# A two-layer decoder trunk on one core: gates read by ScalarE, eleven projections per layer summed in one PSUM bank

## The chip, the cores and the metric

The kernel runs on one core of a Trainium2 chip. TensorE (PE in the profile) multiplies, VectorE (DVE) and ScalarE (ACT) do the elementwise work, GpSimd (POOL) does a little of it, and SyncE (SP) issues most of the transfers. The metric is device time in microseconds (us) of one execution, as the median of several runs. Before the change it is 1203.29 us, the median of 3 runs that lie between 1203.06 and 1203.56.

## The reference

A batch of one sequence of 256 tokens with 1024 channels goes through two layers, in fp32. What matters here:

```python
for l in range(2):
    h = h + 0.5 * swiglu(rms_norm(h, ffn1_norm[l]), ...)          # 1024 -> 2816 -> 1024
    h = h + mixer(rms_norm(h, mix_norm[l]), ...)                   # four head groups, below
    h = h + cross_attention(rms_norm(h, ...), rms_norm(mem, ...))  # 4 heads of 256
    h = h + 0.5 * swiglu(rms_norm(h, ffn2_norm[l]), ...)
return rms_norm(h, final_norm)

def mixer(u):
    z = u @ w_in
    qa, ka, va, oa, ia, fa, pb, qc, kc, vc, qd, kd, vd = split(z)  # 256 wide, ia and fa 4 wide
    # mLSTM: q, k = silu(causal_conv4([qa | ka]));  i = ia + b;  f = log_sigmoid(fa + b);
    #        chunked recurrence over q, k, va, normalised, times sigmoid(oa)
    # pool:  trailing-window means of pb, minus pb, a 64x64 map per group
    # dilated attention on qc, kc, vc;  differential attention on qd, kd, vd
    return concat([ya, yb, yc, yd]) @ w_out
```

Cross attention needs `K` and `V` from `mem`; the kernel computes these inside the mixer's stretch.

## The kernel before, in words

**Weights.** All weights lie in one array, in the order in which they are used, cut into slabs of 128 x 1024 numbers (1040 where four gate columns are added). SP loads a slab into a `raw` tile. ScalarE copies it, rounded, into the high half of a `whl` tile (the cast, L221), and VectorE puts the remainder into the low half (L222). There are five `whl` buffers, so the cast of a slab needs the buffer of the slab five places earlier, and waits until TensorE has made the last product with that. Five slabs are held ahead of or under TensorE, and casts and remainders come in slab order.

**Products.** Activations are kept as a high and a low part too, and a product is high x high + high x low + low x high. `mm2` does it with two matmuls: one 512 columns wide (L366, the weight's high part against both parts of the activation, which fills two halves of a PSUM bank) and one 256 wide (L367). `mm3` does it with three matmuls 256 wide (L360 to L362), all added up in the same 256 columns. The columns streamed are the same, 768.

**Projections.** `proj_T` (L402) computes one unit of 256 output channels or several together: two slabs each, 16 `mm2` each, into a PSUM tile `pj` of two banks. The pool of `pj` tiles has two buffers. After a unit's second slab, `join` adds the two halves: ScalarE copies one half out (L374, tile `jn`), VectorE adds the other (L375), and with that the PSUM tile is free. `proj_M` (L416) does the same with tokens on the partitions; the units `va+ia` and `oa+fa` are 260 columns wide there (L429) and have their last four columns for the gates. Small products go into `pq` tiles, of which there are four.

**The norm.** Rows of a norm are scaled late: `rstd` (L322 ff.) adds up squares (L329), sums them over partitions by matmul (L335), scales on VectorE (`ms`, L339) and takes the power on GpSimd (`r_tok`, L340). `row_bcast` spreads the result over the partitions by two matmuls (L347), and ScalarE copies them out as `rb` (L352). These steps hang in a list, `later`, of which `proj_T` and `proj_M` run one entry after each slab (`flush`). In an FFN's first group the list holds two empty entries, then `rstd`; in the mixer, two empty ones and `rstd`, then, behind the units `qa` and `ka`, the function `go`, which calls `row_bcast` and multiplies `qa` and `ka` by `rb` (L749).

**The mixer's order.** `MIX_ORDER` (L38) is a list of unit and step names in which the program is written: `qa` and `ka` are computed together, then `va+ia`, `oa+fa`, `qd`, `kd`, `vd` and so on; `conv` is the causal convolution of `qa` and `ka` (L829, L832, then Silu on ScalarE, L835), `gates` the log-sigmoid (L844 to L851, with a table load on ScalarE, L845), `rows` the prefix sums by matmul (L858 to L861), `ds`, `df`, `dp` and `cs`, `cf`, `cp` scores, transposes ("flips") and products of the two attentions. A scheduler of the framework then places the instructions of each engine, so an engine's order differs from the written one in places. Within an engine the order is fixed before the run.

**The start.** The channel table `ch` and the four pieces of `x` (tile `h`) come by two DMA queues, and ScalarE loads its first function table (L282). Fourteen matmuls on zeros (L449) precede the first real one.

Of the kernel before, what the change touches and what calls it, by code (L numbers as in the profile page):

```python
# [14 lines left out]
ALU = mybir.AluOpType  # L15
# [21 lines left out]

MIX_ORDER = """qa  ka  va+ia conv  oa+fa gates  qd  kd rows  vd cols  qc mem ms0 ms1 ds0  kc mp0 ms2 ds1 df0  # L38
    vc mp1 ms3 dp0  pb df1 mp2 mp3 mout ds2  K0 pool ds3 dp1 mgain  K1 df2 cs0  K2 mback dp2 df3 cs1 cf0
    K3 dp3 dout cs2 cf1 cp0 pout  V0 dgain cs3 cf2 cp1  V1 dback cf3 cp2  V2 cp3 cout""".split()  # L40

# [202 lines left out]
def trunk(ctx: ExitStack, tc: tile.TileContext, xT, memT, wall, chan, gateb, dlam, t5, poolw, c128, small, out):  # L244
# [156 lines left out]

    def proj_T(units, l, x, evac):  # L402

        ps_ = [pproj() for _ in units]
        for i in range(2):
            for u, p in zip(units, ps_):
                w = W.get(u, l, i, 256)
                for kk in range(4):
                    k = 4 * i + kk
                    for n in range(2):  # L410
                        mm2(p[:, n * 512:n * 512 + 512], parts(w, kk, slice(n * 128, n * 128 + 128)), x(k), k == 0, k == KD - 1)
                flush()
                if i == 1:
                    evac(u, join(p))

# [55 lines left out]
    def ffn(l, name, norm, c_next, extra=()):  # L471
# [218 lines left out]
    def mixer(l, norm, c_next):  # L690
# [43 lines left out]
        def emit(u):  # L734
# [3 lines left out]
            if u in ("qa", "pb"):  # L738
# [20 lines left out]
            elif u in ("qd", "kd", "qc", "kc"):  # L759
# [3 lines left out]
                def ev(_, p):  # L763
# [4 lines left out]
                    else:  # L768
                        V.tensor_tensor(out=pair(t[:, 0:512]), in0=pair(p[:, 0:512]), in1=twice(rb), op=ALU.mult)
                proj_T(["z:" + u], l, xk, ev)  # L770
                z[u] = t
# [10 lines left out]
            elif u == "va+ia":  # L782
# [5 lines left out]
                for b in range(2):  # L788
                    S.activation(out=va[:, b, :, 0:64], in_=o[b][:, 0:256].rearrange("p (a b) -> p a b", a=4), func=AF.Copy,
                                 scale=r[:, b:b + 1])  # L790
                    V.scalar_tensor_tensor(out=ig[:, b, :], in0=o[b][:, 256:260], scalar=r[:, b:b + 1], in1=gb[:, l, 0:4],
                                           op0=ALU.mult, op1=ALU.add)
                z["va"], z["ig"] = va, ig
            else:
# [6 lines left out]
                with tc.high_priority():  # L801
                    for b in range(2):

                        S.activation(out=sg[:, b * 256:b * 256 + 256], in_=o[b][:, 0:256], func=AF.Tanh, scale=rh[:, b:b + 1])
                        V.scalar_tensor_tensor(out=fg[:, b, :], in0=o[b][:, 256:260], scalar=r[:, b:b + 1], in1=gb[:, l, 4:8],  # L805
                                               op0=ALU.mult, op1=ALU.add)
                z["sg"], z["fg"] = sg, fg
# [13 lines left out]

        def mlstm_conv():
            cv = []
            for u, j2 in (("qa", 0), ("ka", 1)):
                c = ztile("cv")
                for a in range(2):
                    j = 2 * j2 + a
                    dst = c[:, a * 256:a * 256 + 256]
                    V.tensor_scalar(out=dst, in0=z[u][:, a, 0:256], scalar1=gcol(cb + C_CONVW, j), scalar2=gcol(cb + C_CONVB, j),  # L829
                                    op0=ALU.mult, op1=ALU.add)  # L830
                    for i in range(1, 4):
                        V.scalar_tensor_tensor(out=dst, in0=z[u][:, a, i:i + 256], scalar=gcol(cb + C_CONVW + 4 * i, j),  # L832
                                               in1=dst, op0=ALU.mult, op1=ALU.add)
                s = ztile("cs")
                S.activation(out=s[:, 0:512], in_=c[:, 0:512], func=AF.Silu)  # L835
                cv.append(s)
            z["qs"], z["ks"] = cv

# [254 lines left out]
        def kv_unit(u):  # L1093
# [5 lines left out]
            if u[0] == "K":  # L1099
                proj_T(["kv:" + u], l, mk, ev)  # L1100
            else:
                ev(u, proj_M("kv:" + u, l, mk, 256))

        steps = {"conv": mlstm_conv, "gates": mlstm_gates, "rows": mlstm_rows, "cols": mlstm_cols, "mout": mlstm_out, "mgain": mlstm_gain, "dgain": diff_gain,
                 "mback": mlstm_back, "dout": diff_out, "dback": diff_back, "cout": dil_out, "pool": pool, "pout": pool_out,
# [127 lines left out]
```

## Time and profile before

| | |
|---|---|
| median of the runs (lowest to highest) | 1203.29 us (1203.06 to 1203.56) |
| the profiled execution, its own time | 1203.03 us |
| its span, first to last instruction | 1201.2 us |
| mean granted TensorE clock, as a share of full speed | 0.998 |
| PE busy | 1185.6 us, 99% |
| DVE busy | 860.1 us, 72% |
| ACT busy | 690.3 us, 57% |
| POOL busy | 55.4 us, 5% |

All times below are microseconds from the start of the span. A line of the timeline gives an instruction's start, its duration, its engine, its line in the kernel, its operation, the tiles it writes and reads, and in brackets how long the engine was idle before it and what ended that. Matmuls overlap: the distance from one start to the next is what a matmul costs, and the duration shown is longer.

### The profile page before, as it was taken

The page shows a single profiled execution, that of the slowest core. Times are in us where ns is not written, and L with a number is a line of the kernel's source. Part 1 is how long each engine was busy: PE and PEld are TensorE (multiplying, and loading weights), DVE is VectorE, ACT ScalarE, POOL GpSimd, SP SyncE. Part 2 cuts the span into 40 slices and gives each one's busy share as a digit, 9 for nine tenths or more (in the row PEclk, how much of TensorE's full clock was granted, in tenths as well). Part 3 has the DMA queues.
Part 4 walks back from the last instruction along what each step waited for, and adds up shares of the span by engine and source line. Part 5 has one row for each costly group of instructions (what it writes and reads, how often), then busy time and mean ns, then how long its engine had stood idle before and what let it go on. Part 6 is the DMA issues. An engine that isn't in the chain of part 4 may idle for free.

```text
span 1201.2 us, 18655 instructions
## 1 busy us (share of the span) xinstructions
PE 1185.6 (99%) x7248; PEld 1048.3 (87%) x7248; DVE 860.1 (72%) x1250; ACT 690.3 (57%) x1035; POOL 55.4 (5%) x69
## 2 busy tenths in 40 slices
PE   8999999999999999999999999999999999999997
PEld 6888888888898988888888888897888999888886
DVE  7787667869667577775677776686785767777653
ACT  7666556556555565554555555555665655655542
POOL 2100000104000000000000000001120000000000
PEclk9999999999999999999999999999999999999999
DMA  8766765554445356666656566655544534555651
GB/s 294 274 212 187 228 189 184 159 175 154 137 152 174 121 193 194 191 183 198 188 181 194 183 194 226 191 177 145 187 142 151 182 124 157 184 195 183 194 191 37
DMA packets 63033, 216.50 MB, mean 180 GB/s; under 512 B 7712, under 2 KB 8112, under 8 KB 62944
## 3 DMA queue, kind: packets, MB, share of 16 engines
q1 hardware_dynamic: 61056, 211.25, 55.3%
q0 software_dynamic: 1024, 2.80, 0.7%
q8 instruction: 57, 0.93, 0.3%
q10 hardware_dynamic: 864, 1.25, 0.3%
q14 instruction: 32, 0.26, 0.1%
HBM read 210.01 MB, written 2.11 MB: 177 GB/s over the span
## 4 chain that ended last, share of the span: by engine, by line
PE 90%; DVE 7%; issue 1%; ACT 1%; DMA 1%; SPq 0%; POOLq 0%; DVEq 0%
PE pj L366 50%; PE pj L367 26%; PE pj L360 3%; PE pj L361 3%; PE pj L362 3%; DVE whl L222 2%; DVE cv L832 1%; ACT whl L221 1%; DMA raw<-in_wall_dram 1%; DVE att L956 1%; PE pq L362 0%; PE pq L360 0%; PE pq L361 0%; PE pq L895 0%; PE pq L966 0%
## 5 line engine op out<-in xcount | busy, mean ns | idle before, releaser
L366 PE MATMUL pj<-xs,whl 128*128 128x512 f32 x1760 | 615.2, 393 | 2.9 <-DVE fg L805 1.7
L222 DVE TENSOR_TENSOR whl<-raw,whl 128x1024 fp32r<-128x1024 f32 (+1 forms) x391 | 473.8, 1215 | 170.4 <-ACT whl L221 165.2
L221 ACT CAST whl<-raw 128x1024 fp32r<-128x1024 f32 (+1 forms) x391 | 406.8, 1042 | 192.5 <-PE pj L367 110.6
L367 PE MATMUL pj<-xs,whl 128*128 128x256 f32 x1760 | 492.6, 280 | 0.2 <-DVE whl L222 0.2
L366 PEld LDWEIGHTS pj<-xs,whl 128*128 128x128 f32 x1760 | 330.3, 188 | 75.3 <-PE pj L367 2.3
L367 PEld LDWEIGHTS pj<-xs,whl 128*128 128x128 f32 x1760 | 332.5, 189 | 1.6 <-issue 0.9
L366 PE MATMUL pj<-fs,whl 128*128 128x512 f32 x660 | 229.2, 392 | 0.0
L374 ACT COPY jn<-pj 128x512 f32<-128x512 f32 x145 | 85.0, 586 | 194.2 <-PE pj L367 194.2
L367 PE MATMUL pj<-fs,whl 128*128 128x256 f32 x660 | 184.7, 280 | 0.0
L375 DVE TENSOR_TENSOR jn<-pj,jn 128x512 f32<-128x512 f32 x145 | 99.9, 689 | 110.1 <-ACT jn L374 109.7
L366 PEld LDWEIGHTS pj<-fs,whl 128*128 128x128 f32 x660 | 123.9, 188 | 27.2
L367 PEld LDWEIGHTS pj<-fs,whl 128*128 128x128 f32 x660 | 124.7, 189 | 0.0
L366 PE MATMUL pj<-whl,ms 128*128 128x512 f32 x128 | 45.9, 400 | 0.0
L366 PE MATMUL pj<-ms,whl 128*128 128x512 f32 x128 | 45.8, 399 | 0.0
L340 POOL TENSOR_TENSOR r_tok<-ms,nhalf 128x2 f32<-128x2 f32 x10 | 7.9, 788 | 800.3 <-DVE ms L339 800.3
L478 ACT ACTIVATE jn<-jn 128x512 f32<-128x512 f32 x44 | 27.8, 633 | 20.0 <-DVE jn L477 19.8
L486 ACT CAST fs<-jn 128x512 fp32r<-128x512 f32 x44 | 27.4, 622 | 19.5 <-DVE jn L483 19.5
L300 ACT ACTIVATE xs<-h,ch 128x256 fp32r<-128x256 f32 x64 | 29.4, 502 | 13.3 <-DVE h L571 8.5
L360 PE MATMUL pj<-ys,whl 128*128 128x256 f32 x128 | 36.1, 282 | 0.3 <-DVE h L571 0.2
L360 PE MATMUL pj<-os,whl 128*128 128x256 f32 x128 | 35.8, 283 | 0.4 <-DVE h L571 0.4
L361 PE MATMUL pj<-os,whl 128*128 128x256 f32 x128 | 35.9, 281 | 0.2
L367 PE MATMUL pj<-whl,ms 128*128 128x256 f32 x128 | 35.9, 280 | 0.0
(269 smaller groups left out, 1361.6 us busy)
## 6 DMA issues: line engine op xcount, KB each, us to landing
raw<-in_wall_dram SPq DMA_DIRECT2D x377, 512.0 KB, 4.0
raw<-in_wall_dram SPq DMA_DIRECT2D x8, 520.0 KB, 3.9
mem<-memd SPq DMA_DIRECT2D x8, 256.0 KB, 4.8
raw<-in_wall_dram SPq DMA_DIRECT2D x6, 256.0 KB, 4.9
mem<-in_memT_dram SPq DMA_DIRECT2D x4, 256.0 KB, 6.9
br<-drow POOLq DMA_DIRECT2D x4, 256.0 KB, 7.3
memd<-mem POOLq DMA_DIRECT2D x4, 256.0 KB, 4.5
qds<-qdh SPq DMA_DIRECT2D x16, 64.0 KB, 2.0
```

Source lines behind the costliest of these rows:

```text
L221: self.nc.scalar.copy(out=hi[:, a:a + m], in_=r[:, a:a + m])
L222: self.last = self.nc.vector.tensor_tensor(out=lo[:, a:a + m], in0=r[:, a:a + m], in1=hi[:, a:a + m].bitcast(F32), op=ALU.subtract)
L300: S.activation(out=hi, in_=src, func=AF.Copy, scale=gcol(c, k))
L360: PE.matmul(o, w(0), x[:, 0, :], start=first, stop=False, skip_group_check=True)
L361: PE.matmul(o, w(0), x[:, 1, :], start=False, stop=False, skip_group_check=True)
L362: PE.matmul(o, w(1), x[:, 0, :], start=False, stop=last, skip_group_check=True)
L366: PE.matmul(o.rearrange("p (s t) -> p s t", s=2), w(0), x, start=first, stop=False, skip_group_check=True)
L367: PE.matmul(o[:, 0:256], w(1), x[:, 0, :], start=False, stop=last, skip_group_check=True)
L374: S.copy(out=tv, in_=v[:, :, 1, :])
L375: V.tensor_tensor(out=tv, in0=v[:, :, 0, :], in1=tv, op=ALU.add)
L478: S.activation(out=gate[:, 0:512], in_=gate[:, 0:512], func=AF.Silu)
L486: S.copy(out=part(f, 0), in_=pair(up[:, 0:512]))
```

## The change

The change has five parts.

1. **Gates.** The four gate columns of `va+ia` and `oa+fa` are read from PSUM by ScalarE (a copy with a scale, two for each unit), and VectorE adds the bias for both token blocks in one instruction from SBUF. Before, two VectorE instructions for each unit read PSUM (L791, L805).
2. **Order of the mixer.** `conv` becomes `cq` (behind `oa+fa`) and `ck` (behind `qd`), with `gates` behind it; `mem` moves behind `kc`; `pool` moves from behind `K0` to behind `K3`, and `pout` behind `V0`.
3. **One bank.** `proj_T` gets `whole=True` for `qa`, `ka`, `pb`, `qd`, `kd`, `qc`, `kc`, `K0` to `K3`, that is for 11 units in each layer: `mm3` instead of `mm2`, both halves of the unit in one bank, and no `join`. What follows reads PSUM: the multiplications by `rb` (L749, L766, L769) and the splits of `K` (L392, L393).
4. **Start.** The table load and the three pieces of `x` on ScalarE's queue keep their written order, `ch`, table, pieces.
5. **FFN.** In the first group of every FFN, `rstd` comes one slab later (three empty entries instead of two).

```diff
-MIX_ORDER = """qa  ka  va+ia conv  oa+fa gates  qd  kd rows  vd cols  qc mem ms0 ms1 ds0  kc mp0 ms2 ds1 df0
+MIX_ORDER = """qa  ka  va+ia  oa+fa cq  qd ck gates  kd rows  vd cols  qc ms0 ms1 ds0  kc mem mp0 ms2 ds1 df0
...
             nc.scalar.dma_start(out=ch[:], in_=chan)
-        q.dma_start(out=h[:, 2 * j:2 * j + 2, :], in_=xT[:, 512 * j:512 * j + 512].rearrange("p (a b) -> p a b", a=2))
+            tc.keep_in_program_order(S.preload_act_table_set("silu_and_others"))
+        tc.keep_in_program_order(q.dma_start(out=h[:, 2 * j:2 * j + 2, :],
+                                             in_=xT[:, 512 * j:512 * j + 512].rearrange("p (a b) -> p a b", a=2)))
         W.load()
-    tc.keep_in_program_order(S.preload_act_table_set("silu_and_others"))
...
-    def proj_T(units, l, x, evac):
+    def proj_T(units, l, x, evac, whole=False):
...
-                        mm2(p[:, n * 512:n * 512 + 512], parts(w, kk, slice(n * 128, n * 128 + 128)), x(k), k == 0, k == KD - 1)
+                        ws = parts(w, kk, slice(n * 128, n * 128 + 128))
+                        if whole:
+                            mm3(p[:, n * 256:n * 256 + 256], ws, x(k), k == 0 and n == 0, k == KD - 1 and n == 1)
+                        else:
+                            mm2(p[:, n * 512:n * 512 + 512], ws, x(k), k == 0, k == KD - 1)
                 flush()
                 if i == 1:
-                    evac(u, join(p))
+                    evac(u, p if whole else join(p))
...
-                later.extend([lambda: None] * 2)
+                later.extend([lambda: None] * 3)
                 later.append(lambda: rbs.append(norm.rstd()))
...
-                proj_T(list(tvs), l, xk, got.__setitem__)
+                proj_T(list(tvs), l, xk, got.__setitem__, whole=True)
...
-                        V.scalar_tensor_tensor(out=fg[:, b, :], in0=o[b][:, 256:260], scalar=r[:, b:b + 1], in1=gb[:, l, 4:8],
-                                               op0=ALU.mult, op1=ALU.add)
+                        S.activation(out=fg[:, b, :], in_=o[b][:, 256:260], func=AF.Copy, scale=r[:, b:b + 1])
+                V.tensor_tensor(out=fg[:], in0=fg[:], in1=gb[:, l:l + 1, 4:8].to_broadcast([128, 2, 4]), op=ALU.add)
...
-        def mlstm_conv():
+        def mlstm_conv(u, j2, name):
```

The new lines shift the numbering: L347 of before is L348 after, L352 is L353, L360 to L362 are L361 to L363, L429 is L435, L749 is L755.

The first place is the passage from `qa` and `ka` to `va+ia` in layer 0. On TensorE before, behind the last product of `ka` (L366, L367), the first 24 matmuls of `va+ia` stand ahead of the two that spread the norm:

```order
L366 MATMUL pj<-xs,whl 128x512
L367 MATMUL pj<-xs,whl 128x256
L366 MATMUL pj<-xs,whl 128x512
L367 MATMUL pj<-xs,whl 128x256
L429 MATMUL pj<-whl,xs 128x260 x24
L347 MATMUL pq<-cc,r_tok 128x128 x2
L429 MATMUL pj<-whl,xs 128x260 x72
```

and now:

```order
L361 MATMUL pj<-xs,whl 128x256
L362 MATMUL pj<-xs,whl 128x256
L363 MATMUL pj<-xs,whl 128x256
L348 MATMUL pq<-cc,r_tok 128x128 x2
L435 MATMUL pj<-whl,xs 128x260 x96
```

The two spreading matmuls (L347, now L348) have moved ahead of all matmuls of `va+ia` and `oa+fa` (96 for both).

On ScalarE at the same place before, with the casts of weights for `oa+fa` (1040 wide) and `qd` (the first 1024 wide one behind them), the joins of `qa` and `ka`, and `rb`:

```order
L221 CAST whl<-raw 128x1040 x2
L300 ACTIVATE xs<-h,ch 128x256 x2
L323 ACTIVATE sq<-h 128x512
L221 CAST whl<-raw 128x1040
L374 COPY jn<-pj 128x512
L221 CAST whl<-raw 128x1040
L374 COPY jn<-pj 128x512
L221 CAST whl<-raw 128x1024 x2
L352 COPY rb<-pq 128x256
```

and now:

```order
L221 CAST whl<-raw 128x1040 x2
L301 ACTIVATE xs<-h,ch 128x256 x2
L324 ACTIVATE sq<-h 128x512
L221 CAST whl<-raw 128x1040 x2
L221 CAST whl<-raw 128x1024
L353 COPY rb<-pq 128x256
L221 CAST whl<-raw 128x1024
```

The joins are gone, and one cast for `qd` still stands ahead of `rb`.

On VectorE at the same place before, from the norm's `ms` to the convolution:

```order
L339 TENSOR_SCALAR ms<-pq 128x2
L800 TENSOR_SCALAR rh<-r_tok 128x2
L375 TENSOR_TENSOR jn<-pj,jn 128x512
L222 TENSOR_TENSOR whl<-raw,whl 128x1040
L375 TENSOR_TENSOR jn<-pj,jn 128x512
L222 TENSOR_TENSOR whl<-raw,whl 128x1024 x2
L749 TENSOR_TENSOR qa<-jn,rb 128x2x256
L749 TENSOR_TENSOR ka<-jn,rb 128x2x256
```

and now:

```order
L340 TENSOR_SCALAR ms<-pq 128x2
L806 TENSOR_SCALAR rh<-r_tok 128x2
L222 TENSOR_TENSOR whl<-raw,whl 128x1040
L222 TENSOR_TENSOR whl<-raw,whl 128x1024
L755 TENSOR_TENSOR qa<-pj,rb 128x2x256
L755 TENSOR_TENSOR ka<-pj,rb 128x2x256
L222 TENSOR_TENSOR whl<-raw,whl 128x1024
```

The multiplications that take `qa` and `ka` out of PSUM now stand behind one remainder for `qd` instead of two, and the joins ahead of them are gone.

The second place is VectorE in the first group of the first FFN, where `jn` is first the gate unit, then the up unit. Before:

```order
L222 TENSOR_TENSOR whl<-raw,whl 128x1024 x2
L329 TENSOR_TENSOR acc<-acc 128x256
L375 TENSOR_TENSOR jn<-pj,jn 128x512
L339 TENSOR_SCALAR ms<-pq 128x2
L222 TENSOR_TENSOR whl<-raw,whl 128x1024
L375 TENSOR_TENSOR jn<-pj,jn 128x512
L222 TENSOR_TENSOR whl<-raw,whl 128x1024 x2
L477 TENSOR_TENSOR jn<-jn,rb 128x512
```

and now:

```order
L222 TENSOR_TENSOR whl<-raw,whl 128x1024 x2
L376 TENSOR_TENSOR jn<-pj,jn 128x512
L222 TENSOR_TENSOR whl<-raw,whl 128x1024
L330 TENSOR_TENSOR acc<-acc 128x256
L376 TENSOR_TENSOR jn<-pj,jn 128x512
L340 TENSOR_SCALAR ms<-pq 128x2
L222 TENSOR_TENSOR whl<-raw,whl 128x1024 x2
L483 TENSOR_TENSOR jn<-jn,rb 128x512
```

The sum of squares (`acc`) and `ms` have moved behind one more remainder and behind the joins.

## Rows read from the trace of the kernel before

**Rows 1.** The page, part 1: busy us (share of the span) and instructions

```profile
PE 1185.6 (99%) x7248; PEld 1048.3 (87%) x7248; DVE 860.1 (72%) x1250; ACT 690.3 (57%) x1035; POOL 55.4 (5%) x69
```

**Rows 2.** Waits of PE: us in total, times, longest

```profile
PE pj L366 <- DVE fg L805: 1.7, 2, 0.8
PE pq L966 <- DVE nm L956: 1.3, 2, 0.7
```

**Rows 3.** Timeline of PE, last slab of ka (mm2): start, duration, operation

```profile
206.62 0.40 PE L366 MATMUL pj<-xs,whl 128*128 128x512 f32 x1
...
208.71 0.39 PE L366 MATMUL pj<-xs,whl 128*128 128x512 f32 x1
...
209.05 3.04 PE L429 MATMUL pj<-whl,xs 128*128 128x260 f32 x24
211.93 0.61 PE L347 MATMUL pq<-cc,r_tok 128*128 128x128 f32 x4
212.29 1.93 PE L429 MATMUL pj<-whl,xs 128*128 128x260 f32 x14
```

**Rows 4.** Timeline of PE, output projection (mm3)

```profile
332.44 0.28 PE L362 MATMUL pj<-ys,whl 128*128 128x256 f32 x1
...
335.57 0.28 PE L362 MATMUL pj<-ys,whl 128*128 128x256 f32 x1
...
337.70 0.28 PE L362 MATMUL pj<-ys,whl 128*128 128x256 f32 x1
```

**Rows 5.** Timeline of ACT behind ka

```profile
209.25 0.59 ACT L374 COPY jn<-pj 128x512 f32<-128x512 f32 x1 [1.68 <-PE pj L367]
...
212.17 1.05 ACT L221 CAST whl<-raw 128x1024 fp32r<-128x1024 f32 x1 [1.38 <-issue]
213.13 0.36 ACT L352 COPY rb<-pq 128x256 f32<-128x256 f32 x1
```

**Rows 6.** Timeline of DVE behind ka

```profile
213.25 1.22 DVE L222 TENSOR_TENSOR whl<-raw,whl 128x1024 fp32r<-128x1024 f32 x1 [1.20 <-ACT whl L221]
214.40 0.69 DVE L749 TENSOR_TENSOR qa<-jn,rb 128x512 f32<-128x512 f32 x1
```

**Rows 7.** Timeline of PE, from qd to kd in layer 0

```profile
226.44 0.28 PE L367 MATMUL pj<-xs,whl 128*128 128x256 f32 x1
227.57 0.47 PE L366 MATMUL pj<-xs,whl 128*128 128x512 f32 x1 [0.85 <-DVE fg L805]
```

**Rows 8.** Timeline of PE, at a flip of layer 0

```profile
297.90 0.28 PE L367 MATMUL pj<-ms,whl 128*128 128x256 f32 x1
298.85 0.55 PE L966 MATMUL pq<-cc,e 128*128 128x128 f32 x3 [0.67 <-DVE nm L956]
```

**Rows 9.** Timeline of ACT, the gates' table load in layer 0

```profile
227.19 1.28 ACT L845 ACT_TABLE_LOAD   x1
```

**Rows 10.** Timeline of PE, first group of the first FFN

```profile
19.30 0.28 PE L367 MATMUL pj<-xs,whl 128*128 128x256 f32 x1
20.22 0.58 PE L335 MATMUL pq<-ones,acc 128*128 128x1 f32 x4 [0.65 <-ACT jn L374]
...
23.62 0.60 PE L347 MATMUL pq<-cc,r_tok 128*128 128x128 f32 x4
```

**Rows 11.** Timeline of DVE in the same stretch

```profile
17.39 2.35 DVE L222 TENSOR_TENSOR whl<-raw,whl 128x1024 fp32r<-128x1024 f32 x2
```

**Rows 12.** Timeline of POOL in the same stretch

```profile
21.15 1.56 POOL L340 TENSOR_TENSOR r_tok<-ms,nhalf 128x2 f32<-128x2 f32 x1 [19.41 <-DVE ms L339]
```

**Rows 13.** Timeline of ACT at the start

```profile
5.22 0.51 ACT L300 ACTIVATE xs<-h,ch 128x256 fp32r<-128x256 f32 x1 [1.31 <-DMA ch<-in_chan_dram]
6.23 0.62 ACT L221 CAST whl<-raw 128x512 fp32r<-128x512 f32 x1 [0.50 <-DMA raw<-in_wall_dram]
```

**Rows 14.** Timeline of PE at the start, matmuls on zeros

```profile
1.32 2.31 PE L449 MATMUL pj<-warm 128*128 128x512 bf16 x5 [1.32 <-POOL nhalf L291]
...
4.95 1.24 PE L449 MATMUL pj<-warm 128*128 128x512 bf16 x5
```

More of the change, by code (lines that the diff above doesn't have):

```diff
@@ L36 @@
 OUT_ORDER = [0, 1, 2, 3, 6, 7, 4, 5]
-MIX_ORDER = """qa  ka  va+ia conv  oa+fa gates  qd  kd rows  vd cols  qc mem ms0 ms1 ds0  kc mp0 ms2 ds1 df0
-    vc mp1 ms3 dp0  pb df1 mp2 mp3 mout ds2  K0 pool ds3 dp1 mgain  K1 df2 cs0  K2 mback dp2 df3 cs1 cf0
-    K3 dp3 dout cs2 cf1 cp0 pout  V0 dgain cs3 cf2 cp1  V1 dback cf3 cp2  V2 cp3 cout""".split()
+MIX_ORDER = """qa  ka  va+ia  oa+fa cq  qd ck gates  kd rows  vd cols  qc ms0 ms1 ds0  kc mem mp0 ms2 ds1 df0
+    vc mp1 ms3 dp0  pb df1 mp2 mp3 mout ds2  K0 ds3 dp1 mgain  K1 df2 cs0  K2 mback dp2 df3 cs1 cf0
+    K3 pool dp3 dout cs2 cf1 cp0  V0 dgain cs3 cf2 cp1 pout  V1 dback cf3 cp2  V2 cp3 cout""".split()
 C_PER_LAYER = 66
@@ L769, in ev @@
                         V.tensor_tensor(out=pair(t[:, 0:512]), in0=pair(p[:, 0:512]), in1=twice(rb), op=ALU.mult)
-                proj_T(["z:" + u], l, xk, ev)
+                proj_T(["z:" + u], l, xk, ev, whole=True)
                 z[u] = t
@@ L790, in emit @@
                                  scale=r[:, b:b + 1])
-                    V.scalar_tensor_tensor(out=ig[:, b, :], in0=o[b][:, 256:260], scalar=r[:, b:b + 1], in1=gb[:, l, 0:4],
-                                           op0=ALU.mult, op1=ALU.add)
+                    S.activation(out=ig[:, b, :], in_=o[b][:, 256:260], func=AF.Copy, scale=r[:, b:b + 1])
+                V.tensor_tensor(out=ig[:], in0=ig[:], in1=gb[:, l:l + 1, 0:4].to_broadcast([128, 2, 4]), op=ALU.add)
                 z["va"], z["ig"] = va, ig
@@ L820, in group_rms @@
             return rs
-        def mlstm_conv():
[L823 to L837, printed above, removed]
+        def mlstm_conv(u, j2, name):
+            c = ztile("cv")
+            for a in range(2):
+                j = 2 * j2 + a
+                dst = c[:, a * 256:a * 256 + 256]
+                V.tensor_scalar(out=dst, in0=z[u][:, a, 0:256], scalar1=gcol(cb + C_CONVW, j), scalar2=gcol(cb + C_CONVB, j),
+                                op0=ALU.mult, op1=ALU.add)
+                for i in range(1, 4):
+                    V.scalar_tensor_tensor(out=dst, in0=z[u][:, a, i:i + 256], scalar=gcol(cb + C_CONVW + 4 * i, j),
+                                           in1=dst, op0=ALU.mult, op1=ALU.add)
+            s = ztile("cs")
+            S.activation(out=s[:, 0:512], in_=c[:, 0:512], func=AF.Silu)
+            z[name] = s
         def mlstm_gates():
@@ L1099, in kv_unit @@
             if u[0] == "K":
-                proj_T(["kv:" + u], l, mk, ev)
+                proj_T(["kv:" + u], l, mk, ev, whole=True)
             else:
                 ev(u, proj_M("kv:" + u, l, mk, 256))
-        steps = {"conv": mlstm_conv, "gates": mlstm_gates, "rows": mlstm_rows, "cols": mlstm_cols, "mout": mlstm_out, "mgain": mlstm_gain, "dgain": diff_gain,
+        steps = {"cq": lambda: mlstm_conv("qa", 0, "qs"), "ck": lambda: mlstm_conv("ka", 1, "ks"), "gates": mlstm_gates, "rows": mlstm_rows, "cols": mlstm_cols, "mout": mlstm_out, "mgain": mlstm_gain, "dgain": diff_gain,
                  "mback": mlstm_back, "dout": diff_out, "dback": diff_back, "cout": dil_out, "pool": pool, "pout": pool_out,
```

1 line of the change is left out of this document (removed).

## Prediction

> **What bounds the kernel now.** I read the page's first part first: TensorE is busy 99% of the span, VectorE 72%, ScalarE 57% [rows 1]. So a microsecond is gained or lost only where TensorE waits, or where it issues more. Next the list of what TensorE waits for: the two entries that the change can touch come twice each, once for each layer: a matmul of a projection behind the forget gate `fg`, and a flip behind the row maxima `nm` of the differential scores [rows 2]. Last the timelines around those places and around the places where the order of instructions has changed. TensorE's own rate is read as distances between starts: six `mm2` of `ka`'s last slab run from 206.62 to 208.71, 0.348 us each [rows 3]; fifteen `mm3` of the output projection from 332.44 to 337.70, 0.351 each, the last six of them, from 335.57, 0.355 each [rows 4].
>
> The sum is made for the profiled execution, 1203.03 us (span 1201.2 and 1.8 around it). The median shown, 1203.29, lies 0.26 above it, and that is added at the end. A difference under 0.2%, 2.4 us, I count as no change.
>
> **Part by part, in the order of their weight.**
>
> *One bank, and what it holds up.* The joins go: 11 copies and 11 additions per layer on ScalarE and VectorE. That is work beside TensorE, and worth nothing unless one of them was late. But a join also freed a `pj` tile early. For ten of the eleven units what follows is an instruction that is ready to read PSUM at once, and only one unit at a time holds a buffer. `qa` and `ka` differ: they are computed together, hold both buffers of the pool, and their reader, L749, needs `rb`, the spread norm. In the kernel before, `join` has released `ka` by the addition that follows the copy at 209.25 [rows 5], `va+ia` starts without a gap at 209.05 in the buffer of `qa`, the spreading matmuls run inside it at 211.93 [rows 3], and `qa` is only multiplied at 214.40 [rows 6], out of `jn`, where nothing is held up. In the changed kernel `va+ia` needs the buffer of `qa`, so all its matmuls wait for that multiplication. The order agrees: the two spreading matmuls now stand ahead of the first of them.
>
> How long that takes: ScalarE learns of the end of `ka` at 209.25, when its copy starts [rows 5]. That copy is gone, and what starts at that moment is the cast of the first slab of `qd`: the five `whl` buffers make it wait for just this slab of `ka`. It stands ahead of `rb`, and VectorE's remainder for it stands ahead of the multiplication.
> - cast, 1.05 [rows 5]: to 210.30
> - remainder, which starts 0.03 behind a cast's end (212.17 and 1.05 against 213.25) and lasts 1.22 [rows 5, 6]: to 211.55
> - multiplication of `qa`, which starts 0.07 before the end of the remainder ahead of it, and lasts 0.69 [rows 6]: 211.48 to 212.17; `rb` (0.36, behind the cast) is ready by then
> - the first matmul of `va+ia`: some 0.04 later, 212.21, where it was 209.05.
>
> Of these 3.16 us the two spreading matmuls take 0.36, from 211.93 to 212.29, which they took before too, inside `va+ia` [rows 3]. So TensorE stands still for 2.8 us longer than before. This hits each layer once: **+5.5 us** with 2.75 each. Bounds: if `rb` were served first, it would still need the way from the spreading matmuls to its copy, 211.93 to 213.13 [rows 3, 5], 0.36 for the copy and 0.69 for `qa`: from 209.2 to about 211.5, a stall of some 2.0 less the matmuls, 1.9 a layer. From above, another remainder ahead of it would make it 2.8 + 1.2 = 4.0. So 3.8 to 8.0 for both, and I take 5.5, which the order as it stands gives.
>
> *Three matmuls for two.* Each unit has 16 products, so 11 units have 176 in a layer and 352 in all. By the 15 products of [rows 4] one costs 0.003 us more, by the last six 0.007: +1.0 to +2.5 us. I take **+1.3**, near the longer count. The weight loads of the third matmul lie under the one before, as in [rows 4], where three loads run with three matmuls.
>
> *Gates.* A gap in [rows 7]: 226.44 to 227.57 is 1.13 where 0.12 is normal, 1.01 lost, in both layers [rows 2]. `kd` waits there for the buffer of `oa+fa`, which VectorE frees late: its reads of the gates stand behind the convolution and two remainders, and hold up ScalarE's second half of `oa` as well. Now ScalarE alone frees it, while `qd` (5.6 us of products) runs. **−2.0 us**; nothing of it stays, since 5.6 us are a lot against two short reads and a cast of 1.05. The price of the same edit is that the log-sigmoid comes later: `gates` now stands behind `ck`, whose Silu must come before the table load of 1.28 [rows 9]. By my count of VectorE's and ScalarE's orders behind that, `lf` is ready about 25.6 us after `va+ia` starts, and the matmul that reads it, in the midst of `vd`, is reached after 25.4. This is an estimate from durations like those of [rows 5, 6]; I put +0.25 a layer, **+0.5** (0 to 1.2).
>
> *The flip.* From 297.90 to 298.85 TensorE loses 0.83 [rows 8], in both layers [rows 2], because VectorE does a remainder (as long as in [rows 6], 1.22) and a join before the row maxima that free a `pq` tile. The join of `K` is gone, an addition as long as the multiplication of [rows 6], 0.69, and the pool's multiplications come later. What is late next are the row sums and copies for the same flip, ready about when TensorE wants them. **−1.5** for both (0 to −1.7).
>
> *The FFN's norm one slab later.* In the first FFN, TensorE waited at 19.30 for the sum of squares: 20.22 less 19.30 and less the normal 0.12 is 0.80. With the sum later, it goes on to the next slab, but that starts the second half of the gate unit's buffer turn: it waits for the gate unit's join, now behind two remainders that end at 19.74 [rows 11]. TensorE goes on at about 20.4, and after nine more matmuls (1.57) stands at the column sums at 21.95. From there to the end of the power on GpSimd took 20.22 to 22.71 before, 2.49 us [rows 10, 12], the power alone 1.56. So `r_tok` is there at 24.44, and the spreading matmuls, which now follow only seven matmuls later, start at 24.48 instead of 23.62 [rows 10]: **+0.86**. In the other three FFNs GpSimd's power is short (the waits list has no entry for it), and the wait is hidden by seven or eight products: 0, up to +1.2 in each if VectorE takes one remainder first. I keep 0 as the value and 1.2 for the range.
>
> *Order of the start.* ScalarE waits for `ch` until 5.22 in any case, and then for a weight piece 0.50 [rows 13]. The table load fits before that; the pieces of `x` are issued 1.28 later (a table load's duration, [rows 9]) and have slack by my reading of their arrivals. 0, between −0.5 (the weights' first pieces come sooner) and +1.28.
>
> *Pool and `mem`.* They move work of VectorE, GpSimd and the transfer queue across a stretch where no wait of TensorE is listed other than the flip. 0.
>
> **Sum:** 5.5 + 1.3 − 2.0 + 0.5 − 1.5 + 0.9 = +4.7. 1203.03 + 4.7 = 1207.7; against the median 1203.29, 1208.0. Its own range goes from the stall's lower bound, 1.7 less, and `lf` in time, 0.5 less (1205.8), to a second remainder and dearer products, 2.5 + 1.2 more, cut to 1211 since both at once are unlikely.
>
> **The rivals.**
> - *The new stall isn't there, and the waits are gone.* If `va+ia` starts on time, 1203.29 + 4.7 − 5.5 = 1202.5, no change; if `mm3` costs no more than `mm2` too and the first FFN loses nothing, 1200.3, faster by 0.25%. For it: the waits of [rows 2] do end with what the change takes away. Against it: two tiles in a pool of two, both read only after `rb`. It decides by whether the first matmul of `va+ia` runs before L755 has read `qa`. Chance 0.05 for faster.
> - *A short stall.* ScalarE and VectorE get to `rb` and `qa` sooner than the order suggests, by the lower bound of 1.9 a layer, and `lf` comes in time: 1208.0 − 1.7 − 0.5 = 1205.8, and with the flip fully hidden 1205.6, about the edge of no change. Chance 0.13.
> - *The clock falls in the new gap.* [...] Against it: the longest gaps inside the work before, 1.0 us [rows 7], cost nothing beyond themselves, and the mean clock of the run is 0.998; but no gap of 2.8 us is there to read. [...] Chance 0.10.
>
> **Chances.** The forecast with its range 0.72, a short stall 0.13, the clock 0.10, faster 0.05. The short stall's time is at the edge of no change, and I leave most of it there. So slower by over 0.2%: 0.82; within 0.2%: 0.13; faster: 0.05. The range goes from 1205.2, which leaves out the first rival and part of the second, to 1211.6, which takes in the clock.
>
> **What would show it.** In the timeline of the changed kernel the first L435 behind the last slab of `ka` has an idle time of 2.5 to 3 us in both layers, ended by VectorE's L755; the starts of `mm3` products of `qa` lie 0.351 to 0.355 apart; no wait behind `fg` ahead of `kd`; at the flips no wait, or one of a tenth; the first L348 starts near 24.5. If the gap behind `ka` is missing or under 1.5 us, or TensorE's matmuls behind it are twice as far apart as elsewhere, the forecast is wrong. If the time comes out below 1205 with the gap there, then a gain that I put at 0 was not nothing, most likely among the casts and remainders that the joins delayed.

## The result: 1215.04 us, slower by 1%

| | before | changed |
|---|---|---|
| median (lowest to highest) | 1203.17 us (1203.02 to 1203.56, 4 runs) | 1215.04 us (1214.72 to 1216.25, 4 runs) |
| profiled execution, its span | 1203.03 us, 1201.2 | 1215.22 us, 1213.4 |
| mean granted TensorE clock | 0.998 | 0.995 |

The ratio is 1.0099 (95% interval 1.0086 to 1.0111). The direction was forecast, the size was not: +11.9 us against +4.7, outside the range.

The page's first part for the changed kernel, which answers to [rows 1]:

```profile
PE 1190.4 (98%) x7600; PEld 1067.9 (88%) x7600; DVE 850.1 (70%) x1224; ACT 678.5 (56%) x1021; POOL 53.9 (4%) x69
```

VectorE and ScalarE have 10 and 12 us less to do, and TensorE 352 instructions more, the third matmul of each product. TensorE is busy for 4.8 us more, and its idle time (span less busy time) grew from 15.6 to 23.0. The list of its waits, in place of [rows 2]:

```profile
PE pj L435 <- DVE qa L755: 5.4, 2, 2.7
PE pq L861 <- DVE lf L854: 4.5, 2, 2.3
PE pq L348 <- POOL r_tok L341: 1.8, 2, 1.1
PE pj L367 <- DVE jn L376: 1.5, 1, 1.5
```

The two old entries, `fg` and the row maxima, are gone. In their place stand the wait for `qa` that the prediction named, a wait for `lf` of nearly the same size that it put at a quarter of a microsecond a layer, and two waits of the first FFN. (Of the 1.8 for `r_tok`, 1.1 is the final norm's and stood there before as well.)

**The gap behind `ka`.** TensorE's timeline in layer 0, at the place of [rows 3]:

```profile
210.43 0.28 PE L363 MATMUL pj<-xs,whl 128*128 128x256 f32 x1
210.55 0.61 PE L348 MATMUL pq<-cc,r_tok 128*128 128x128 f32 x4
213.85 0.36 PE L435 MATMUL pj<-whl,xs 128*128 128x260 f32 x1 [2.69 <-DVE qa L755]
```

The four records of the spreading (two matmuls) start at 210.55 and take 0.11 each; the first matmul of `va+ia` follows 2.96 behind the last of them, so 2.85 are lost, and as much in layer 1. ScalarE and VectorE in that time, in place of [rows 5] and [rows 6]; ScalarE first:

```profile
210.79 1.04 ACT L221 CAST whl<-raw 128x1024 fp32r<-128x1024 f32 x1 [2.22 <-PE pj L363]
211.75 0.36 ACT L353 COPY rb<-pq 128x256 f32<-128x256 f32 x1
```

then VectorE:

```profile
211.87 1.23 DVE L222 TENSOR_TENSOR whl<-raw,whl 128x1024 fp32r<-128x1024 f32 x1 [1.67 <-ACT whl L221]
213.01 0.69 DVE L755 TENSOR_TENSOR qa<-pj,rb 128x512 f32<-128x512 f32 x1
```

Cast, remainder, multiplication, first matmul: the chain of the prediction, link by link.

**The clock behind the gap.** The same stretch by windows of TensorE (microseconds, PE busy and matmul count, granted clock, DMA share, GB/s), with the gap of layer 1 below:

```profile
205.00:210.00 5.00, 5.00 (x46) 1.00 0.62 202
210.00:213.80 3.80, 1.16 (x11) 1.00 0.47 152
213.80:217.80 4.00, 3.95 (x20) 0.57 0.38 131
217.80:221.40 3.60, 3.60 (x32) 1.00 0.02 5
...
804.90:807.70 2.80, 0.12 (x2) 1.00 0.59 187
807.70:811.60 3.90, 3.89 (x20) 0.57 0.39 137
```

In the 4 us behind the gap the granted clock is 0.57, a mean of two levels: it is 0.50 from 214.3 to 217.7 (in layer 1 from 808.2 to 811.6) and 1.00 before and behind that. So 20 matmuls of `va+ia` pass in these 4 us, where the next 3.6 us, at 1.00, have 32. That is the rival that had a chance of 0.10. Between 214.3 and 217.7 the starts lie 0.217 apart instead of 0.12, which loses 1.5 us, 3.0 for both layers. An idle stretch of 2.85 us was enough for it here.

**The wait for `lf`.** TensorE in layer 0, in the midst of `vd`:

```profile
240.62 0.39 PE L367 MATMUL pj<-whl,xs 128*128 128x512 f32 x1
243.24 0.59 PE L861 MATMUL pq<-cc,lf 128*4 128x256 f32 x2 [2.23 <-DVE lf L854]
```

2.62 from start to start, 2.5 of it lost; 2.6 in layer 1. VectorE's instructions that lead there:

```profile
235.04 1.71 DVE L833 TENSOR_SCALAR cv<-ka,ch 128x256 f32<-128x256 f32 x2
236.67 2.45 DVE L836 SCALAR_TENSOR_TENSOR cv<-ka,ch,cv 128x256 f32<-128x256 f32 x6
239.05 1.21 DVE L222 TENSOR_TENSOR whl<-raw,whl 128x1024 fp32r<-128x1024 f32 x1
240.18 0.68 DVE L775 TENSOR_TENSOR kd<-pj,rb 128x512 f32<-128x512 f32 x1
242.05 1.13 DVE L854 SCALAR_TENSOR_TENSOR lf<-fg,na 128x8 f32<-128x8 f32 x1 [1.19 <-ACT na L852]
```

ScalarE's part of the chain:

```profile
239.16 0.63 ACT L839 ACTIVATE cs<-cv 128x512 f32<-128x512 f32 x1 [2.52 <-DVE cv L836]
239.81 1.28 ACT L848 ACT_TABLE_LOAD   x1
241.10 0.21 ACT L849 ACTIVATE na<-na 128x8 f32<-128x8 f32 x1
241.22 0.60 ACT L732 CAST kdh<-kd 128x512 fp32r<-128x512 f32 x1
241.72 0.30 ACT L852 ACTIVATE na<-na,ones 128x8 f32<-128x8 f32 x1
```

and GpSimd's subtractions for the low parts of `qd` and `kd`:

```profile
234.46 1.82 POOL L733 TENSOR_TENSOR qdl<-qd,qdh 128x512 fp32r<-128x512 f32 x1 [25.61 <-ACT qdh L732]
241.90 1.27 POOL L733 TENSOR_TENSOR kdl<-kd,kdh 128x512 fp32r<-128x512 f32 x1 [5.62 <-DMA qds<-qdl]
```

Two rows of VectorE are about 1 us too long. The two `TENSOR_SCALAR` of a convolution take 0.73 for `qa` (226.51 in this trace) and 1.71 here; `lf`, eight numbers a partition, took 0.15 before and takes 1.13. Both start behind an instruction of GpSimd and end when that ends: the first `TENSOR_SCALAR` at about 236.4 (GpSimd at 234.46 + 1.82 = 236.28), `lf` at 243.18 (241.90 + 1.27 = 243.17). Layer 1 has the same lengths, 1.72 and 1.13, and both end as GpSimd's instruction does, to 0.15 us. That it is GpSimd's instruction which holds VectorE's up is a reading of these rows; without it, in e4, they take 0.73 and 0.16. By what means it does so no run shows.

**The first FFN**, in place of [rows 10]:

```profile
18.96 0.28 PE L368 MATMUL pj<-xs,whl 128*128 128x256 f32 x1
20.70 0.50 PE L367 MATMUL pj<-xs,whl 128*128 128x512 f32 x1 [1.47 <-DVE jn L376]
...
22.43 0.50 PE L336 MATMUL pq<-ones,acc 128*128 128x1 f32 x4
...
24.89 0.71 PE L348 MATMUL pq<-cc,r_tok 128*128 128x128 f32 x4 [0.70 <-POOL r_tok L341]
```

TensorE comes to this place 0.34 earlier than before (18.96 against 19.30), waits 1.63 for the gate unit's join and 0.86 for `r_tok`.

**The sum**, from the two traces, in us of the profiled executions (12.18 in all): the first `qa` starts at 198.79 instead of 197.51, +1.28 for start and FFN; gaps behind `ka` +5.7; clock behind them +3.0; waits for `lf` +5.1; waits behind `fg` −2.0; at the flips −1.65; products +1.2 (352 times some 0.0035: products of one-bank units start 0.351 apart on average, those of two banks 0.3475). These are 12.6; the 0.4 by which they are too much lies in smaller differences that no run takes apart. As a check, from the first `qa` to the output projection the two layers take 137.25 and 137.27 instead of 131.76 and 131.90, 10.9 more, where the terms without start and FFN make 11.3.

### The profile page after: what moved, and what is told of

The parts are those of the page before. It is cut to its first block, busy times and chain, and to the rows that moved or that the text cites. A ratio compares the mean times of both kernels' runs of the same rounds, so it can differ in the third digit from the quotient of the medians.

```text
span 1213.4 us, 19343 instructions
## 1 busy us (share of the span) xinstructions
PE 1190.4 (98%) x7600; PEld 1067.9 (88%) x7600; DVE 850.1 (70%) x1224; ACT 678.5 (56%) x1021; POOL 53.9 (4%) x69
## 3 DMA queue, kind: packets, MB, share of 16 engines
q0 software_dynamic: 1024, 2.80, 0.8%
q10 hardware_dynamic: 864, 1.25, 0.3%
## 4 chain that ended last, share of the span: by engine, by line
PE 93%; DVE 3%; ACT 1%; DMA 1%; issue 1%; POOL 0%; SPq 0%; POOLq 0%; DVEq 0%; ACTq 0%
PE pj L367 44%; PE pj L368 23%; PE pj L361 6%; PE pj L362 6%; PE pj L363 6%; PE pj L435 2%; DVE whl L222 1%; DMA raw<-in_wall_dram 1%; ACT whl L221 1%; PE pq L951 1%; PE pq L363 0%; PE pq L969 0%; PE pq L361 0%; PE pq L362 0%; PE pq L950 0%
## 5 line engine op out<-in xcount | busy, mean ns | idle before, releaser
L367 PE MATMUL pj<-xs,whl 128*128 128x512 f32 x1536 | 535.9, 393 | 1.7 <-DVE jn L376 1.5
L368 PE MATMUL pj<-xs,whl 128*128 128x256 f32 x1536 | 430.0, 280 | 0.2 <-DVE whl L222 0.2
L367 PEld LDWEIGHTS pj<-xs,whl 128*128 128x128 f32 x1536 | 288.3, 188 | 65.0 <-DVE jn L376 1.8
L368 PEld LDWEIGHTS pj<-xs,whl 128*128 128x128 f32 x1536 | 290.2, 189 | 1.5 <-issue 0.9
L367 PE MATMUL pj<-fs,whl 128*128 128x512 f32 x660 | 229.2, 392 | 0.0
L375 ACT COPY jn<-pj 128x512 f32<-128x512 f32 x123 | 72.1, 586 | 168.1 <-PE pj L368 168.1
L376 DVE TENSOR_TENSOR jn<-pj,jn 128x512 f32<-128x512 f32 x123 | 84.9, 690 | 90.8 <-ACT jn L375 90.1
L367 PEld LDWEIGHTS pj<-fs,whl 128*128 128x128 f32 x660 | 123.9, 188 | 27.2
L361 PE MATMUL pj<-xs,whl 128*128 128x256 f32 x224 | 63.1, 282 | 0.0
L363 PE MATMUL pj<-xs,whl 128*128 128x256 f32 x224 | 62.7, 280 | 0.0
L362 PE MATMUL pj<-xs,whl 128*128 128x256 f32 x224 | 62.7, 280 | 0.0
L367 PE MATMUL pj<-whl,ms 128*128 128x512 f32 x128 | 45.9, 400 | 0.0
L363 PEld LDWEIGHTS pj<-xs,whl 128*128 128x128 f32 x224 | 42.3, 189 | 0.0
L361 PEld LDWEIGHTS pj<-xs,whl 128*128 128x128 f32 x224 | 42.1, 188 | 0.1
L362 PEld LDWEIGHTS pj<-xs,whl 128*128 128x128 f32 x224 | 42.1, 188 | 0.0
```

Source lines behind the costliest of these rows:

```text
L361: PE.matmul(o, w(0), x[:, 0, :], start=first, stop=False, skip_group_check=True)
L362: PE.matmul(o, w(0), x[:, 1, :], start=False, stop=False, skip_group_check=True)
L363: PE.matmul(o, w(1), x[:, 0, :], start=False, stop=last, skip_group_check=True)
L367: PE.matmul(o.rearrange("p (s t) -> p s t", s=2), w(0), x, start=first, stop=False, skip_group_check=True)
L368: PE.matmul(o[:, 0:256], w(1), x[:, 0, :], start=False, stop=last, skip_group_check=True)
L375: S.copy(out=tv, in_=v[:, :, 1, :])
```

## The experiments

Twelve kernels, each timed beside the kernel before on the same chip. There the kernel before took 1204.01 us (e1 to e4), 1203.44 (e5 to e8) and 1203.40 (e9 to e12), so kernels of different groups are better compared by their ratios than by their medians. e4, e5 and e12 leave out the low parts of `qd` and `kd`, and with them a part of the differential scores: they are there to measure, and are no replacement.

| run | median us | ratio to before (95%) | granted clock |
|---|---|---|---|
| changed kernel | 1215.04 | 1.0099 (1.0086 to 1.0111) | 0.995 |
| e1, `qa`, `ka` joined | 1208.62 | 1.0035 (1.0022 to 1.0048) | 0.995 |
| e2, one tile for both | 1208.85 | 1.0037 (1.0022 to 1.0052) | 0.996 |
| e3, gap filled | 1214.19 | 1.0084 (1.0066 to 1.0102) | 0.995 |
| e4, no GpSimd subtraction | 1209.24 | 1.0040 (1.0025 to 1.0055) | 0.995 |
| e5, e2 and e4 | 1202.68 | 0.9995 (0.9986 to 1.0004) | 0.997 |
| e6, three empty entries only | 1204.66 | 1.0009 (1.0000 to 1.0018) | 0.998 |
| e7, gates only | 1199.55 | 0.9969 (0.9957 to 0.9980) | 0.998 |
| e8, combined | 1201.88 | 0.9988 (0.9979 to 0.9997) | 0.997 |
| e9, one bank only | 1209.10 | 1.0047 (1.0033 to 1.0061) | 0.994 |
| e10, gates and start | 1199.08 | 0.9967 (0.9955 to 0.9980) | 0.998 |
| e11, gates and order | 1203.60 | 1.0001 (0.9992 to 1.0010) | 0.997 |
| e12, e4 with the gap filled | 1207.32 | 1.0033 (1.0021 to 1.0045) | 0.997 |

The clock is that of the profiled execution.

### e1: qa and ka with joins

```diff
-                proj_T(list(tvs), l, xk, got.__setitem__, whole=True)
+                proj_T(list(tvs), l, xk, got.__setitem__, whole=u == "pb")
```

> The changed kernel with qa and ka alone back on two banks and the joins; the other nine units per layer stay in one bank. Theory (two tiles held until rb): va+ia starts without a gap, so 5.7 us of waiting go, and with the gap the fall of the clock behind it, 3.3 us: 1215.0 - 9.0 = about 1206.0; the wait for lf stays near 2.5 a layer. Rival (the clock falls for another reason, such as the density of the 260-wide matmuls): only the gap goes, about 1209.3. Rival (the order behind qa and ka shifts and the wait only moves): 1212 or more.

1208.62, 2.6 above the theory and near the first rival. The gaps behind `ka` are gone. The waits for `lf` are the same (2.63 and 2.72 from start to start), but now the clock falls behind *them*:

```profile
205.00:211.00 6.00, 6.00 (x39) 1.00 0.59 180
236.00:238.70 2.70, 0.53 (x3) 1.00 0.41 97
238.70:242.70 4.00, 3.93 (x16) 0.63 0.43 105
```

So the fall belongs to neither place: in each layer of this trace TensorE loses 2.5 us or more at one place, and the clock falls behind it.

### e2: one tile for qa and ka

```diff
-        ps_ = [pproj() for _ in units]
+        if whole and len(units) == 2:
+            both = pproj()
+            ps_ = [both[:, 512 * j:512 * j + 512] for j in range(2)]
+        else:
+            ps_ = [pproj() for _ in units]
```

> The changed kernel with qa and ka summed in the two banks of one PSUM tile, so that the second tile is free for va+ia; no join for either. Theory: as in the run before, no gap and no fall of the clock, about 1206.0, and it shows that it is the number of tiles held, not the missing join. Rival (reading qa and ka late still holds up oa+fa, the next user of that tile): a shorter gap of about 1 us a layer ahead of oa+fa, about 1208.

1208.85. Without a join, and with one tile of the pool left for `va+ia`, the gap is gone. With joins (e1) it goes as well, so what made it was the number of tiles held until `rb` is there. The rival's short wait is there too, one in each layer ahead of `oa+fa`:

```profile
216.92 0.47 PE L439 MATMUL pj<-whl,xs 128*128 128x260 f32 x2 [0.41 <-DVE ka L759]
```

0.69 from start to start, 0.57 lost. The clock falls behind the wait for `lf` in layer 0 and stays up in layer 1, behind a gap as long:

```profile
236.60:239.00 2.40, 0.19 (x1) 0.95 0.41 98
239.00:243.00 4.00, 3.97 (x16) 0.60 0.46 109
...
828.20:830.70 2.50, 0.21 (x1) 1.00 0.44 103
830.70:834.70 4.00, 3.97 (x24) 1.00 0.47 112
```

### e3: the gap behind ka filled

```diff
                 def go():
+                    rstd()
+                    if u == "qa":
+                        pf = psmall()
+                        for _ in range(14):
+                            PE.matmul(pf[:, 0:384], identb[:], maskb[:], start=True, stop=True)
                     for n_, p in got.items():
```

> The changed kernel with 14 matmuls on constants (384 columns, results unused) put in between the spreading of the norm and va+ia, some 2.3 us of the 2.85 us gap in each layer. Theory (idle TensorE lowers the clock): va+ia starts at the same time, but runs at the upper level: 3.3 us less, about 1211.7, granted clock 1.00 behind the gap. Rival (the clock falls with the change of work, not with idleness): unchanged, 1215. Rival (the fillers delay va+ia): 1215 to 1217.

1214.19, hardly less than the changed kernel. By itself that looks like the rival. The windows tell another story: behind the filled gap the clock stays at 1.00, and it falls behind the wait for `lf`, which was not filled.

```profile
210.50:213.30 2.80, 2.38 (x16) 1.00 0.57 186
213.30:217.30 4.00, 4.00 (x33) 1.00 0.41 137
238.60:241.10 2.50, 0.33 (x2) 0.97 0.43 103
241.10:245.10 4.00, 3.92 (x15) 0.59 0.47 110
```

### e4: no subtraction on GpSimd

```diff
-            hi, lo = ztile(u + "h", F32R), ztile(u + "l", F32R)
+            hi = lo = ztile(u + "h", F32R)
...
-            G.tensor_tensor(out=lo[:, 0:512], in0=t[:, 0:512], in1=hi.bitcast(F32)[:, 0:512], op=ALU.subtract)
```

> The changed kernel without GpSimd's low parts of qd and kd (the transfers send the high parts in their place, so that part of the products of the differential scores is left out). Theory (GpSimd's subtraction blocks VectorE's convolution of ka and its lf for about 1 us each): lf comes 2 us earlier, the wait at the prefix sums falls from 2.5 to about 0.5 a layer: 1215.0 - 4.0 = about 1211. Rival (lf is late because of where the convolution and the table load stand): the wait stays over 2 us a layer, 1214 or more.

1209.24, 5.8 less than the changed kernel (7 by the ratios), where 4 were expected. The wait for `lf` is gone altogether, which is 5.1, and in the trace the clock falls behind the gap of layer 0 and not behind that of layer 1:

```profile
213.20:217.20 4.00, 3.94 (x20) 0.58 0.44 131
...
804.70:808.70 4.00, 3.99 (x33) 1.00 0.39 131
```

The 96 matmuls of `va+ia` and `oa+fa` take 13.06 in layer 0 and 11.58 in layer 1, which is the price of one fall again, 1.5. VectorE's two rows have the lengths that they have where GpSimd is idle:

```profile
232.73 0.73 DVE L832 TENSOR_SCALAR cv<-ka,ch 128x256 f32<-128x256 f32 x2
233.37 2.46 DVE L835 SCALAR_TENSOR_TENSOR cv<-ka,ch,cv 128x256 f32<-128x256 f32 x6
...
240.16 0.16 DVE L853 SCALAR_TENSOR_TENSOR lf<-fg,na 128x8 f32<-128x8 f32 x1
```

That is 2 us of the 2.5. The rest has another cause: with GpSimd's instructions gone the scheduler put the convolution of `ka` ahead of a remainder (1.22) behind which it stood. So the run shows that the blocking costs 2 us a layer, and not that it is the only reason.

### e5: neither gap

The edits of e2 and e4 together.

> The changed kernel with both edits: qa and ka in one PSUM tile, and no low parts of qd and kd from GpSimd (the transfers send the high parts instead; a part of the differential scores is left out). Theory (the clock falls once a layer behind whichever of the two gaps is there): both gaps are gone, and the fall with them: 1215.0 - 5.7 - 5.1 - 3.3 + 0.9 (the short wait for ka's read) = about 1202, with no granted clock under 1.00 between the start and the end. Rival (the clock falls for some other reason in this stretch): it still falls, about 1205.

1202.68 against 1203.44 for before on the same chip. TensorE has no gap over 0.7 us between the first FFN and the final norm, and the granted clock is 1.00 there. By the ratios it is 12.5 us below the changed kernel. Together with e1 to e4 this settles it: the loss is the two gaps, and the clock behind them.

### e6: three empty entries

```diff
-                later.extend([lambda: None] * 2)
+                later.extend([lambda: None] * 3)
```

> The kernel before with three empty entries instead of two in the first group of each FFN, nothing else. Theory (the later norm costs twice in the first FFN, at the gate unit's join and at r_tok, and nothing in the other three): 1203.2 + 1.2 to 1.7 = about 1204.6. Rival (it costs in the other three FFNs too): 1206 or more. Rival (no cost; what was lost there comes from the order of the start): 1203.2.

1204.66, +1.2 against 1203.44, at the low end of the theory (the interval of the ratio reaches from 0 to 2.2 us). Both waits of the first FFN are in its trace; the other three FFNs have none.

### e7: the gates only

The hunks of the change on `ig` and `fg`, applied to the kernel before.

> The kernel before with the gates read by ScalarE alone, nothing else; convolutions, order and joins as before. Theory (ScalarE frees the buffer of oa+fa in time): the two waits behind fg go, 2.0 us: about 1201.3, and no new wait at the prefix sums, since the convolution of ka still stands early. Rival (ScalarE's Tanh of oa stands behind the Silu of ka, which keeps half of the wait): about 1202.3.

1199.55, ratio 0.9969: twice the expected gain. The waits behind `fg` are gone, and those at the flips with them. No join has gone in this kernel, so the flip's wait was not the join's doing alone. In its trace VectorE's order ahead of the flip of layer 0 is another: the join (296.85) follows the two scalings of `e` directly, where in the kernel before a remainder of 1.21 (296.05) stands between them. On the flip the prediction had the right size for a wrong, or at least not the only, reason.

### e8: what is left of the change, combined

The changed kernel with e2's tile, two empty entries, and

```diff
-MIX_ORDER = """qa  ka  va+ia  oa+fa cq  qd ck gates  kd rows  vd cols  ...
+MIX_ORDER = """qa  ka  va+ia cq  oa+fa ck gates  qd  kd rows  vd cols  ...
```

> What the runs so far leave of the change: gates read by ScalarE, one bank for 11 units with qa and ka in one tile, the start's order, the new places of pool and mem; but two empty entries in the FFN as before, the convolution of qa behind va+ia, that of ka and the gates behind oa+fa. Theory: the gains stay (fg 2.0, flip 1.7, start 0.3) without the gaps, less 0.9 for ka's read and 0.4 for the products: 1203.2 - 2.7 = about 1200.5. Rival (the gates' chain is late again at the prefix sums): 1203 or more.

1201.88. No gap, but 2.3 us more than e7: from the first `qa` to the output projection layer 0 takes 131.15 us here and 129.75 in e7. 0.57 of these 1.4 is the wait for `ka`'s read, 0.6 the products (176 times 0.0035). So one bank has a price, and no gain is to be seen once the gates are off VectorE. e8 also has `ck` behind `oa+fa` and the new places of `pool` and `mem`, and no run tells these apart.

### e9: one bank only

The hunks of the change on `proj_T` and its calls, applied to the kernel before.

> The kernel before with one bank for the 11 units of each layer (qa and ka in two tiles, as in the changed kernel), nothing else. Theory (this part alone makes the gap behind ka): 1203.3 + 5.7 (gaps) + up to 3.3 (clock) + 0.4 (products) = 1209.5 to 1212.7, with the waits behind fg still there. Rival (without the joins VectorE catches up, and the waits behind fg and at the flip go as well): 3.7 less, 1206 to 1209.

1209.10. The theory's gap is there, and so is the fall of the clock in both layers; the rival's relief is there too. The wait list has one entry of the mixer left:

```profile
PE pj L433 <- DVE qa L753: 5.4, 2, 2.7
```

The 96 matmuls behind the gaps take 13.10 and 12.87 where 11.6 is normal, 2.8 for the clock. With 1203.4 + 5.7 + 2.8 + 1.2 − 3.7 the terms make 1209.4, 0.3 above what was measured. No wait for `lf` is there.

### e10: gates and start

> The kernel before with the gates read by ScalarE and the start's new order, nothing else. Theory (the two are independent, the start gives 0.3 to 0.4): ratio to before as in the run with the gates alone (0.9969) less 0.0003, about 1199.2 where before takes 1203.3. Rival (the first FFN waits for its own data and takes the gain back): 1199.6.

1199.08, the fastest of all. Its ratio and e7's lie well within each other's intervals, so the start's gain is not settled by the times; in the traces, the last matmul ahead of the first wait in the FFN starts at 19.08 here and at 19.37 in e7.

### e11: gates and the new order of convolutions

> The kernel before with the gates read by ScalarE and the convolutions and gates in the changed order (cq behind oa+fa, ck and gates behind qd), with joins, old places of pool and mem, old start and FFN. Theory (the later convolution of ka makes lf late, blocked further by GpSimd): a gap of about 2.5 us a layer at the prefix sums and, in most runs, the fall of the clock behind it: 1199.6 + 5 + up to 3.3 = 1204.6 to 1208. Rival (the late lf needs the one-bank units too): 1200 to 1201.

1203.60, 3.9 more than e7 by the ratios, but by another way than forecast. The wait for `lf` is 0.9 from start to start, not 2.5: the units still have joins, `kd` comes out later, GpSimd starts on it at 239.83, and `lf` at 238.29 is not blocked (0.16). The convolution of `ka` is: 1.72 for its two `TENSOR_SCALAR` from 230.91, where GpSimd is at the subtraction for `qd` from 230.59 to 232.15. And the waits at the flips are back, with 1.18 and 1.25. The clock stays up (1.00 in the mixers of both layers). So the new order costs by itself, at both places, and among these runs the long wait for `lf` stands only where the new order, one bank and GpSimd's subtractions come together. The rival came nearer in mechanism, neither in size.

### e12: e4 with the gap behind ka filled

> The changed kernel without GpSimd's low parts of qd and kd (a part of the differential scores is left out, as in the run before with that edit), so that the gap behind ka is the only one, and that gap filled with 14 matmuls on constants. Theory (the clock falls because TensorE idles): va+ia starts as late as without them, but at the upper level in both layers: 1209.2 less 1.7 to 3.3 = 1206 to 1207.6. Rival (the fall has another cause): 1209.2, with granted clock near 0.6 behind the gap.

1207.32, with e4 at 1209.24 on another chip. TensorE starts `va+ia` as late as in e4:

```profile
210.43 2.44 PE L757 MATMUL pq<-maskb,identb 128*128 128x384 bf16 x14
213.28 0.95 PE L435 MATMUL pj<-whl,xs 128*128 128x260 f32 x6 [0.41 <-DVE qa L759]
```

and the clock stays up behind the filled gap, where e4's fell in layer 0:

```profile
210.00:213.30 3.30, 2.89 (x21) 1.00 0.50 163
213.30:217.00 3.70, 3.70 (x31) 1.00 0.45 146
```

The 96 matmuls behind it take 11.58, where e4's took 13.06 in layer 0: matmuls whose results nobody reads bought 1.5 us there. The ratios alone don't show it (their intervals overlap), but all six runs of e12 have a mean clock of 0.997 or 0.998, all four of e4 0.995. Over the traces of the changed kernel, e4 and e9 the clock fell behind five of the six open gaps behind `ka`; in e3 and e12 it fell behind none of the four filled ones. In these runs it is idleness that lowers the clock.

## Why the prediction was wrong, point by point

Two terms failed. The larger is the late `lf`, +0.5 in the sum and +5.1 in the trace: alone it would have made 1212.6, outside the range. The other is the clock, which was left out of the sum and cost 3.0: alone it would have made 1211.0, still inside.

- *Gates, the late `lf`: the term that was mis-sized,* +0.5 against +5.1. The place and the chain (convolution, Silu, table load, `lf`) were right, and so was most of the count: `lf` was to be ready 25.6 us behind the start of `va+ia`. Measured are 29.3, of which 1.5 is the slow clock, which holds up TensorE as well. Another 2 are two instructions of VectorE that GpSimd blocked for 1 us each, as e4 shows. The durations were taken from [rows 5, 6] and the like, from stretches where GpSimd is idle, and moving the convolution behind `qd` brought it beside GpSimd's subtraction. The prediction named GpSimd's work only where `pool` and `mem` move.
- *The clock: the rival came true.* It was given 0.10, and the range ends at 1211.6 to take it in, 3.6 above the forecast's 1208.0: no run shows that term; the trace of the changed kernel shows 3.0, with the granted clock at 0.50 for 3.4 us behind each gap. The step that failed was "the longest gaps inside the work before, 1.0 us, cost nothing beyond themselves": that says nothing of gaps of 2.85, and the forecast took it as a reason to leave the clock out of the sum. The prediction's own sign, matmuls twice as far apart behind the gap, came: 0.217 instead of 0.12. e3 and e12 show the cause.
- *One bank, and what it holds up: right.* 5.5 was said, 5.7 measured, with the chain as worked out; e9 shows that this part alone makes the gap, and e2 that it is the two tiles. (The lower bound of 1.9 a layer is 2.1 by its own rows, 211.5 less 209.05 and less 0.36; nothing hangs on it.)
- *Gates, the gain: right,* −2.0, in e7 and in the changed kernel.
- *The flip: right in size, by luck.* It goes in e7 without any join removed, it goes in e9 with the joins removed and the gates untouched, and it stays in e11. VectorE's order there differs from kernel to kernel; what settles it stays open.
- *Three matmuls for two: right,* 0.0035 us a product, 1.2 in all.
- *The FFN: right in kind.* +0.86 was said for the spreading; it starts at 24.89 instead of 23.62, +1.27, and since the start came 0.34 sooner the FFN itself lost 1.6 in this trace. e6 alone makes it 1.2. The gate unit's join let TensorE go on at 20.70, 0.3 later than worked out, and that wait is not steady: 1.2 to 2.1 from start to start in the traces with three empty entries.
- *The start: right,* 0 was said, −0.34 is in the trace, within its bounds; the times of e10 and e7 don't settle it.

With the terms as measured the sum is 12.6 for the 12.2 of the profiled executions: what was missing were one certain cost, in a stretch whose neighbour engine wasn't looked at, and a rival whose condition (a gap far longer than any in the trace) was part of the forecast itself.

## What to carry to other kernels

When a unit's consumer must wait for a late value, count the buffers that are held until then before taking away the step that freed them. When an instruction moves, read its new neighbours on the other engines, not only those on its own queue: beside GpSimd's subtraction two instructions of VectorE took 1 us longer here. And when a forecast makes a gap longer than any in the trace, the clock behind it belongs in the sum with a real chance: the trace has no row against it. Here the fall came behind ten of fourteen gaps of 2.5 us and more (in the traces of the changed kernel, e1 to e4 and e9), and behind `ka` it cost 1.3 to 1.5 us each time.

## What was unexpected of the hardware

In the layers that have such a gap, the granted clock mostly fell once, behind whichever gap of 2.5 to 2.85 us came first, and not behind the second one, 27 us later (the changed kernel: behind `ka`, not behind `lf`). It is not certain for a gap of that size: e2 kept 1.00 behind 2.6 us in layer 1, and e4 behind 2.85 in layer 1, where each lost it in layer 0. What decides between the two cases at equal length stays open. Behind the gaps of the first FFN (up to 2.08 from start to start) and the short ones of the mixer it fell in none of these traces (1.00). At the final norm, where two gaps of 1.3 us have only 0.4 us of small matmuls between them, it had fallen before the last spreading in e4, e9 and e11 (0.50 throughout the 4 us that hold it). An instruction of VectorE on eight numbers a partition took 1.13 us instead of 0.15 beside one of GpSimd on 512.
